# One tuned two-layer encoder kernel: the openings' PSUM bank pairs, the norm's scaled copy, the split of the late row tile and the first down group are changed

## Chip, cores and metric

The kernel runs on one core of a Trainium2 chip. The metric is the device time of one execution in microseconds (us), as the median of several runs. The engines are named as the profile names them: PE (TensorE, matmul), DVE (VectorE), ACT (ScalarE), POOL (GpSimd) and SP (SyncE, which here only issues DMAs).

## What is computed

512 frames and 16 meta tokens (528 tokens of 1024 channels, fp32) pass two layers; each layer is a half-weighted SwiGLU FFN, a mixer and a second FFN. Cut to what matters here:

```python
def swiglu(x, w_gate, w_up, w_down):
    return (jax.nn.silu(x @ w_gate) * (x @ w_up)) @ w_down
...
    for l in range(DEPTH):
        h = h + 0.5 * swiglu(rmsnorm(h, ffn1_norm[l]), ffn1_w_gate[l], ffn1_w_up[l], ffn1_w_down[l])
        h = h + hybrid_mixer(rmsnorm(h, mix_norm[l]), w_in[l], ...)
        h = h + 0.5 * swiglu(rmsnorm(h, ffn2_norm[l]), ffn2_w_gate[l], ffn2_w_up[l], ffn2_w_down[l])
    h = rmsnorm(h, final_norm)
    return h[:, N_META:]
```

The mixer projects to q, k, v, two convolution halves a and b, and two gates; it runs a stick-breaking attention and a causal depthwise convolution and merges both. D_FF is 2816, so an FFN has 22 row tiles of 128 hidden channels.

## The kernel before

**Precision.** Activations lie transposed, 128 channels by 528 tokens a tile. Every fp32 operand is split into a high part (a cast to fp32r, by ScalarE, line 80) and a low part (the difference, by VectorE, line 81); a product is three matmuls: high by high, high by low, low by high. Weights arrive by DMA as `wr` (256 to 512 KB each) and are split into `wh` and `wl`, four buffers each, in `prep_unit` (lines 254 to 289). `unit` (291) hands out the split weights in the order in which TensorE uses them and splits `LOOK` = 3 units ahead. For most units of the mixer the low part is made in another way (lines 265 to 268): ScalarE writes the cast, then a negated copy of the raw weight's part, and a DMA on POOL's queue adds to it; only q's first weight tile takes the plain split.

**Order.** A scheduler orders each engine's instructions ahead of time by priorities; `priority(-URGENT)` moves something forward, and a manual dependency without a semaphore only fixes an order on one engine. `follow` (249) uses such a dependency to keep a weight split behind the last instruction that TensorE waits for, kept in `ahead`. Within openings and first down groups TensorE's order is written by hand.

**Openings.** Products of pairs of row tiles use seven products in place of eight (a 2 by 2 block scheme over token halves and channel halves; w11, s1, s2, w21, s3, w22, s4). The first two pairs of an FFN, and a and b in the mixer, are interleaved in `pair` (lines 438 to 540): five openings in all, two in mixers and three in FFNs (the first FFN has a head of its own, `first_head`). PSUM has eight banks, used as four pairs under the tags ps (two), pb and pe. An opening begins with o11 for both row-tile pairs (`As`), while the norm's sum of squares is still being finished; it copies the first result into pb (`begin`), and lets TensorE form the norm's column sums (`between`, `rms_rstd`, 558). `rsqrt` (549) then makes the reciprocal root: Ln and Exp on ScalarE give a first value, and one Newton step on VectorE uses a scaled copy of the sums (line 553). After that come o21, s1, s2, o21, w22, s3, s1, s2, s4, s3, w22, s4. `evict` (677), or `take` in the mixer (956), empties a PSUM pair: gate by rstd, silu or sigmoid, up by gate.

**Down products.** After the first 4, 10, 16 and 22 row tiles an FFN runs `down` (799): eight output tiles in the order 0, 4, 1, 5, 2, 6, 3, 7, each a sum over the group's row tiles. Only the last group's result goes straight to h; the others are scaled by rstd on VectorE (816) and added by POOL (818). A row tile whose product came out last waits in `late`; its split (`parts`, 642) is done at the start of `down`. So that TensorE has something to do meanwhile, the first two or, after an opening, three output tiles are begun together and take the late row tiles last (lines 821 to 835).

Of the kernel before, what the change touches and what calls it, by code (L numbers as in the profile page):

```python
# [61 lines left out]
def kernel(ctx, tc, hT, par, const, wg1, wu1, wd1, win, wao, wco, wout, wg2, wu2, wd2, out):  # L62
# [108 lines left out]
                units += [((f"d{fi}", l, gi, j), wd[l, j, :, m0:m1], m1 - m0) for j in ORDER]  # L171
    LOOK = 3
    RAW = 3
    state = {"prep": 0, "use": 0, "fetch": 0, "out": 0, "sums": 0, "look": LOOK}
    ready, raws, counted = {}, {}, set()
    quads = {"pool": None, "of": None}

# [76 lines left out]
    def prep_unit():  # L254
        n = state["prep"]
        key, src, nk = units[n]
        state["prep"] += 1
        fetch()
        hi = wpool.tile([P, 8, P], F32R, tag="wh", bufs=4, name="wh")
        lo = wpool.tile([P, 8, P], F32R, tag="wl", bufs=4, name="wl")  # L260
        ready[key] = (hi, lo)
        if nk not in QUAD:
            raw, nk0, nk = raws[key], nk, 8 if nk in OPEN else nk
            if key[0] in MIXER and key[0] + str(key[2]) != "q0" or nk0 == "o21" and units[n - 1][2] == "o11":
                act.copy(hi[:, :nk], raw[:, :nk])  # L265
                act.activation(lo[:, :nk], raw[:, :nk], AF.Copy, scale=-1.0)
                for a, b, src in pieces(n):
                    pool.dma_start(lo[:, a:b], src.bitcast(F32R), accum_op=ALU.add)
            else:
                split(raw[:, :nk], hi[:, :nk], lo[:, :nk])  # L270
            drop(key)
        else:
            at = key[1:]
            if at in opened:
                fetch_sums(WHEN.get((nk, units[n - 1][2]), 0))
            elif nk == "w11":
                fetch_sums(2)
            if nk == "s2" or nk == "s4" and at not in opened:
                x, y = raws[("s1", *at)], raws[("w22" if nk == "s2" else "w21", *at)]
                i = dve.tensor_tensor(out=x, in0=x, in1=y, op=ALU.add)  # L280
                if at in opened:
                    follow(i, "dve")
            pair_ = split(raws[("s1" if nk in ("s2", "s4") else nk, *at)], hi, lo)
            if at in opened:
                for i, engine in zip(pair_, ("act", "dve")):
                    follow(i, engine)
            for d in DONE[nk]:
                drop((d, *at))
        fetch()
# [148 lines left out]
    def pair(ptile, sp, st, mode, of, ats, between, take, done):  # L438
# [42 lines left out]
        def out(n, c, i, t):  # L481
            with priority(-URGENT):
                ahead["act"], ahead["dve"] = take(n, c, i, t)

        Bs = [ptile("pb")]
        As = [ptile() for _ in range(2)]
        ahead.clear()
        state["look"] = 1
        ws = [unit("o11", *of, at) for at in ats]
# [2 lines left out]
            products(As[n], ws[n], x(0, 0), True, ks)  # L492
        begin(Bs[0], v(As[0]))
        copy = ahead["act"]
        between(ptile("pe"), copy)

        Bs.append(kept(As[1], False))
        G, q, E, c22 = {}, {}, {}, {}
# [5 lines left out]
        def step(name, n):  # L504
            if (name, n) in (("w22", 0), ("s4", 0)):
                add_w21(int(name == "s4"))
            w = unit(name, *of, ats[n])
            if name == "o21":
                products(As[n], w, x(0, 1))
                (out if n else take)(n, As[n], 0, 0)  # L510
                if n:
                    keep, Bs[n], G[n] = Bs[n], ptile(), ptile()
                    begin(Bs[n], keep)
            elif name == "s1":
                if not n:
                    G[n] = ptile("pe")
                products(G[n], w, sx(0), True)
                q[n] = kept(G[n])
            elif name == "s2":
                products(Bs[n], w, sx(1))  # L520
                E[n] = ptile("pe")
                opposite(E[n], Bs[n], q[n])
            elif name == "s3":
                products(Bs[n], w, sx(2))
                c22[n] = sp.tile([P, 2, TH], F32, tag="c22", bufs=2, name="c22")
                opposite(c22[n], Bs[n], q[n])
                out(n, c22[n], 1, 1)
            elif name == "w22":
                products(E[n], w, sx(3))
                out(n, E[n], 1, 0)  # L530
            else:
                done(n, 1)
                products(Bs[n], w, x(1, 1))
                out(n, Bs[n], 0, 1)
                done(n, 0)
# [22 lines left out]
    def rms_rstd(tp, st, ps, mode, dst=None):  # L558

        if dst is None:  # L560
            dst = npool.tile([P, T], F32, tag="rstd", bufs=1, name="rstd")
        src = st["sum"]
        hi, lo = (tp.tile([P, T], F32R, tag="nt", bufs=3, name="nt") for _ in range(2))
        ahead["act"], ahead["dve"] = split(tri(src, mode), tri(hi, mode), tri(lo, mode))
        for pi, part in enumerate((hi, lo)):
            for b, s, w in ranges(mode):
                pe.matmul(ps[:, b, :w], onesm, part[:, s:s + w], start=(pi == 0), stop=(pi == 1))
        x, y = (tp.tile([P, T], F32, tag="nt", bufs=3, name="nt") for _ in range(2))
        rsqrt(sv(dst, mode), sv(x, mode), sv(y, mode), pv(ps, mode), -D, 1e-6, 0)
        return dst  # L570


# [52 lines left out]
    def ffn(l, fi, st, mode, after):  # L625
# [3 lines left out]
        with tc.tile_pool(name=f"ffn{l}{fi}", bufs=1, reuse_waits="tile") as fp, \  # L629
# [12 lines left out]
            def parts(u, m):  # L642
                if m >= GROUPS[-1][0]:
                    pool.tensor_tensor(out=tri(u, mode), in0=tri(u, mode), in1=tri(norm["r"], mode), op=ALU.mult)
                ah = fp.tile([P, T], F32R, tag="ah", bufs=6, name="ah")
                al = fp.tile([P, T], F32R, tag="al", bufs=6, name="al")
                split(tri(u, mode), tri(ah, mode), tri(al, mode))
                a_parts[m] = (ah, al)

            def plain(tag, key, m, between=None):  # L650

# [61 lines left out]
            def first_head():  # L713

                ws = [tuple(wpool.tile([P, 8, P], F32R, tag=n, bufs=4, name=n) for n in ("wh", "wl")) for _ in begin]
                pss = [ptile(t) for t in ("ps", "ps", "pb")]
                for name in ("s1", "s3"):
                    fetch(quads["pool"].tile([P, 8, P], F32, tag=name, bufs=2, name=name))
                for a, b in BEGIN:
                    for k in range(a, b):  # L720
                        prepare(fp, k, 0, st, alloc="later")
                    for raw, (hi, lo) in zip(begin, ws):
                        split(raw[:, a:b], hi[:, a:b], lo[:, a:b])
                    for k in range(a, b):
                        squares(fp, k, st, mode)
                    if b == KD:
                        fetch()
                        fetch_sums(2)
                        nc.sync.dma_start(prm[:, N_NORM:], par[:, N_NORM:])
                        norm["r"] = npool.tile([P, T], F32, tag="rstd", bufs=1, name="rstd")  # L730
                        rstd_from(fp, st["sum"], ptile("pe"), D, 1e-6, 0, mode, norm["r"])
                    for k in range(a, b):
                        xh, xl = st["u"][k]
                        for ps, (hi, lo) in zip(pss, ws):
                            for pi, (wt, xt) in enumerate(((hi, xh), (hi, xl), (lo, xh))):
                                for e, s in enumerate(toks):
                                    pe.matmul(ps[:, e, :TH], wt[:, k, :], xt[:, s], start=(k == 0 and pi == 0),
                                              stop=(k == KD - 1 and pi == 2))
# [60 lines left out]
            def down(gi, opened=False, tp=None):  # L799
                with priority(-opened * URGENT):  # L800
                    while late:
                        parts(*late.pop())
                m0, m1 = GROUPS[gi]
                last = gi == len(GROUPS) - 1
                xs = [a_parts[m] for m in range(m0, m1)]
                nk = m1 - m0
                tags = ("ps", "ps", "pb", "pe")

                def update(j, pd):
                    if last:  # L810
# [8 lines left out]


                ws, pds = [], []
                if opened:
                    tags = ("ps", "pb", "pe", "ps")
                n0 = 3 if opened else 2
                for n in range(n0):
                    state["look"] = LOOK - n * opened
                    ws.append(unit(f"d{fi}", l, gi, ORDER[n]))
                    pds.append(ptile(tags[n]))
                state["look"] = LOOK
                with tc.manual_schedule(engines={mybir.EngineType.PE}) if opened else nullcontext():  # L830
                    for ks in (range(nk - 2), (nk - 1,), (nk - 2,)):
                        for j in range(n0):
                            gemm(pds[j], ws[j], 0, nk, xs, mode, ks, nk - 2)
                for n in range(n0):
                    update(ORDER[n], pds[n])
                for n, j in list(enumerate(ORDER))[n0:]:
                    if last and after is finish_prepare and n == KD - 2:
                        finish(tp, ptile, [unit(f"d{fi}", l, gi, j) for j in ORDER[n:]], nk, xs)
                        break
                    pd = ptile(tags[n % 4])  # L840
                    gemm(pd, unit(f"d{fi}", l, gi, j), 0, nk, xs, mode)
                    update(j, pd)

# [519 lines left out]
```

## Time and profile before

| | |
|---|---|
| runs, median | 2143.83 us (2143.65 to 2146.93, 3 runs) |
| the profiled execution | 2141.3 us |
| its span, first to last instruction | 2139.5 us |
| granted TensorE clock | 0.999 |
| matmuls | 16058 |
| DMA moved | 334.34 MB, mean 156 GB/s |

The profile is one execution. Its rows give start, length, engine, line of the kernel, operation and `out<-in` by the program's names (buffer numbers left out), the partitions by elements, and in brackets how long the engine had been idle and what ended that. A row with x2 is two instructions merged. Matmul ends are modelled, and matmuls overlap: a matmul of 264 columns has a length of 0.28 us but the next one may start after 0.12. In the mixer's openings the tags ps, pb and pe appear as bs, bb and be.

### The profile page before, as it was taken

The numbers are of one execution on the slowest core, as the hardware profiler recorded it, in microseconds if no ns is written. First come the engines' busy times: TensorE is split into PE (matmuls) and PEld (weight loads), VectorE is DVE, ScalarE is ACT, GpSimd is POOL, SyncE is SP. The second block draws the span as 40 slices with busy tenths as digits, with TensorE's granted clock in tenths as the row PEclk, the third lists the DMA queues.
The fourth block names the chain that finished last, engine by engine and source line by source line (L and its number), as shares of the span: only waits on it lengthen the run. The fifth ranks groups of instructions, "written<-read, shape, count | busy, mean of one in ns | idle before, by whom it ended". The sixth has DMA issues, their size and how long they took to land.

```text
span 2139.5 us, 39983 instructions
## 1 busy us (share of the span) xinstructions
PE 2118.2 (99%) x16058; PEld 2031.1 (95%) x16058; DVE 1600.1 (75%) x2233; ACT 1170.8 (55%) x1660; POOL 514.1 (24%) x477
## 2 busy tenths in 40 slices
PE   9999999999999999999999999999999999999998
PEld 9999999999999999999999999999888889899897
DVE  6867688788876777677797676887788768767685
ACT  6434356677776645343564343566778776444354
POOL 1322321311111141323123223213212112322220
PEclk9999999999999999999999999999999999999999
DMA  7465538665568867464386655385656788665542
GB/s 227 137 165 142 145 104 227 165 134 125 131 172 182 206 169 180 125 164 119 99 210 167 165 144 143 104 223 157 150 121 140 182 186 208 179 178 143 144 110 78
DMA packets 152121, 334.34 MB, mean 156 GB/s; under 512 B 16896, under 2 KB 21120, under 8 KB 151936
## 3 DMA queue, kind: packets, MB, share of 16 engines
q1 hardware_dynamic: 110928, 235.27, 33.9%
q0 software_dynamic: 40320, 95.96, 26.2%
q8 instruction: 126, 2.06, 0.4%
q10 hardware_dynamic: 688, 0.55, 0.1%
q14 instruction: 59, 0.48, 0.1%
HBM read 325.30 MB, written 6.42 MB: 155 GB/s over the span
## 4 chain that ended last, share of the span: by engine, by line
PE 88%; DVE 5%; DMA 4%; ACT 1%; issue 1%; POOL 0%; SPq 0%; DVEq 0%; ACTq 0%; POOLq 0%
PE ps L761 15%; PE pb L761 14%; PE ps L906 13%; PE ps L308 11%; PE ps L892 10%; PE pb L308 6%; PE pe L308 5%; PE pe L761 5%; DMA wl<-win 1%; DVE wl L81 1%; PE ps L459 1%; PE z L1091 1%; PE po L1135 1%; PE z L1114 1%; PE bb L459 1%
## 5 line engine op out<-in xcount | busy, mean ns | idle before, releaser
L80 ACT CAST wh<-wr 128x1024 fp32r<-128x1024 f32 (+4 forms) x296 | 263.8, 898 | 344.8 <-PE ps L308 91.8
L81 DVE TENSOR_TENSOR wl<-wr,wh 128x1024 fp32r<-128x1024 f32 (+4 forms) x296 | 331.5, 1124 | 64.8 <-ACT wh L80 62.3
L80 ACT CAST wh<-s 128x1024 fp32r<-128x1024 f32 x171 | 179.3, 1048 | 261.4 <-DVE s L280 87.4
L81 DVE TENSOR_TENSOR wl<-s,wh 128x1024 fp32r<-128x1024 f32 x171 | 233.0, 1363 | 49.1 <-ACT wh L80 48.0
L818 POOL TENSOR_TENSOR h<-h,dt 128x528 f32<-128x528 f32 (+1 forms) x96 | 176.9, 1850 | 257.2 <-DVE dt L816 256.5
L906 PE MATMUL ps<-uh,wh 128*128 128x264 f32 (+1 forms) x664 | 207.5, 312 | 0.0
L906 PE MATMUL ps<-uh,wl 128*128 128x264 f32 (+1 forms) x664 | 203.7, 307 | 0.7 <-DMA wl<-win 0.7
L906 PE MATMUL ps<-ul,wh 128*128 128x264 f32 (+1 forms) x664 | 203.7, 307 | 0.0
L210 POOL DMA_DIRECT2D s<-wg x81 | 72.0, 889 | 524.9 <-DMA s<-wg 312.8
L935 DVE SCALAR_TENSOR_TENSOR y<-uc,prm,y 128x528 f32<-128x528 f32 (+1 forms) x240 | 184.4, 806 | 0.5
L761 PE MATMUL ps<-ul,wh 128*128 128x264 f32 (+1 forms) x576 | 163.7, 284 | 0.0
L761 PE MATMUL pb<-sl,wh 128*128 128x264 f32 (+1 forms) x576 | 163.3, 283 | 0.0
L761 PE MATMUL ps<-uh,wl 128*128 128x264 f32 (+1 forms) x576 | 163.2, 283 | 0.0
L761 PE MATMUL pb<-sh,wl 128*128 128x264 f32 (+1 forms) x576 | 163.2, 283 | 0.0
L761 PE MATMUL pb<-sh,wh 128*128 128x264 f32 (+1 forms) x576 | 162.9, 283 | 0.0
L761 PE MATMUL ps<-uh,wh 128*128 128x264 f32 (+1 forms) x576 | 162.6, 282 | 0.0
L308 PE MATMUL ps<-ah,wh 128*128 128x264 f32 (+1 forms) x616 | 142.2, 301 | 1.5 <-ACT ah L80 1.5
L308 PE MATMUL ps<-al,wh 128*128 128x264 f32 (+1 forms) x616 | 142.2, 300 | 1.0 <-DVE al L81 0.9
L308 PE MATMUL ps<-ah,wl 128*128 128x264 f32 (+1 forms) x616 | 141.8, 300 | 0.0
L265 ACT CAST wh<-wr 128x1024 fp32r<-128x1024 f32 x91 | 95.4, 1049 | 84.3 <-PE ps L906 36.3
L906 PEld LDWEIGHTS ps<-uh,wl 128*128 128x128 f32 x664 | 125.0, 188 | 7.0 <-DMA wl<-win 1.1
L906 PEld LDWEIGHTS ps<-uh,wh 128*128 128x128 f32 x664 | 124.9, 188 | 5.4
(404 smaller groups left out, 6836.8 us busy)
## 6 DMA issues: line engine op xcount, KB each, us to landing
wr<-wd SPq DMA_DIRECT2D x96, 384.0 KB, 3.6
wr<-wg SPq DMA_DIRECT2D x129, 256.0 KB, 3.1
wr<-wu SPq DMA_DIRECT2D x129, 256.0 KB, 3.6
wr<-win SPq DMA_DIRECT2D x56, 512.0 KB, 3.9
wl<-win POOLq DMA_DIRECT2D x54, 512.0 KB, 7.9
s<-wg SPq DMA_DIRECT2D x87, 256.0 KB, 5.1
s<-wu SPq DMA_DIRECT2D x87, 256.0 KB, 5.5
s<-wg POOLq DMA_DIRECT2D x81, 256.0 KB, 5.1
```

What stands on the lines that cost most here:

```text
L80: i = act.copy(hi, x)
L81: return i, dve.tensor_tensor(out=lo, in0=x, in1=f(hi), op=ALU.subtract)
L210: queue.dma_start(raw[:, a:b], src, **kw)
L265: act.copy(hi[:, :nk], raw[:, :nk])
L308: pe.matmul(ps[:, c, :n], wt[:, k0 + k, :], xt[:, s:s + n], start=(k == 0 and pi == 0), stop=(k == end and pi == 2))
L459: pe.matmul(ps[:, e, :TH], wt[:, 4 * e + kk, :], xt, start=start and kk == 0 and pi == 0, stop=kk == KH - 1 and pi == 2, skip_group_check= ...
L761: pe.matmul(ps[:, e, :TH], wt[:, 4 * e + kk, :], xt, start=start and kk == 0 and pi == 0, stop=kk == 3 and pi == 2, skip_group_check=True)
L818: pool.tensor_tensor(out=tri(h[j], mode), in0=tri(h[j], mode), in1=tri(t, mode), op=ALU.add)
L892: pe.matmul(ps, wt[:, k0 + k, :], xt[:, s], start=(n == 0 and pi == 0), stop=(n == nk - 1 and pi == 2))
L906: pe.matmul(ps, wt[:, k, :], xt[:, s], start=(n == 0 and pi == 0), stop=(n == KD - 1 and pi == 2))
L935: t = dve.scalar_tensor_tensor(out=y, in0=uc[i][:, c0 + k:k + T], scalar=col(w0 + k), in1=y, op0=ALU.mult, op1=ALU.add)
L1091: pe.matmul(z[:, hh, :n], kk[r, ks], qq[r, q0:q0 + n], start=(pi == 0), stop=False, skip_group_check=True)
```

## The change

- **Bank pairs.** In `pair` the first opening tile moves from ps to pe, the norm's sums from pe to ps, s1's and s2's result tiles from pe to ps, and the copied tile of the second row-tile pair from ps to pe. `down` uses the pairs in the order ps, ps, pb, pe, also after an opening; the last group uses ps, ps, pe, pb. `first_head` names pb and pe before ps.
- **Norm.** `rms_rstd` no longer calls `rsqrt`: the scaled copy of the sums is made by ScalarE, from PSUM, between Ln and Exp, with the factor 0.5; the constants of the Newton step are arranged to fit. Other users of `rsqrt` are as before.
- **Late row tile.** `parts` returns the two instructions of its split; `down` keeps them in `ahead`, and weight units that are split while the first tiles of an opened down group are requested follow behind them.
- **First down group.** It begins three output tiles together in every FFN, the first FFN too; there the row tiles come in the order 0, 1, then 2, then 3.
- **k's first weight tile** takes the plain split. **s3's eviction** in an opening is no longer urgent and no longer what later splits follow.

```diff
@@ prep_unit
-            if key[0] in MIXER and key[0] + str(key[2]) != "q0" or nk0 == "o21" and units[n - 1][2] == "o11":
+            if key[0] in MIXER and key[0] + str(key[2]) not in ("q0", "k0") or nk0 == "o21" and units[n - 1][2] == "o11":
...
-                split(raw[:, :nk], hi[:, :nk], lo[:, :nk])
+                pair_ = split(raw[:, :nk], hi[:, :nk], lo[:, :nk])
+                if state["behind"]:
+                    for i, engine in zip(pair_, ("act", "dve")):
+                        follow(i, engine)
@@ pair
-        As = [ptile() for _ in range(2)]
+        As = [ptile(), ptile("pe")][::-1]
...
-        between(ptile("pe"), copy)
+        between(ptile(), copy)
...
-                    keep, Bs[n], G[n] = Bs[n], ptile(), ptile()
+                    keep, Bs[n], G[n] = Bs[n], ptile("pe"), ptile()
...
-                    G[n] = ptile("pe")
+                    G[n] = ptile()
...
-                E[n] = ptile("pe")
+                E[n] = ptile()
...
-                out(n, c22[n], 1, 1)
+                take(n, c22[n], 1, 1)
@@ rms_rstd
-        rsqrt(sv(dst, mode), sv(x, mode), sv(y, mode), pv(ps, mode), -D, 1e-6, 0)
+        r, x, y, ps = sv(dst, mode), sv(x, mode), sv(y, mode), pv(ps, mode)
+        fn(r, ps, AF.Ln, bias=bias[:, 0:1], scale=-1.0 / D)
+        act.activation(x, ps, AF.Copy, scale=0.5 / D)
+        fn(r, r, AF.Exp, bias=B_ZERO, scale=-0.5)
+        dve.tensor_tensor(out=y, in0=r, in1=r, op=ALU.mult)
+        dve.scalar_tensor_tensor(out=y, in0=x, scalar=-0.5e-6, in1=y, op0=ALU.add, op1=ALU.mult)
+        dve.scalar_tensor_tensor(out=r, in0=y, scalar=1.5, in1=r, op0=ALU.add, op1=ALU.mult)
@@ parts
-                split(tri(u, mode), tri(ah, mode), tri(al, mode))
                 a_parts[m] = (ah, al)
+                return split(tri(u, mode), tri(ah, mode), tri(al, mode))
@@ first_head
-                pss = [ptile(t) for t in ("ps", "ps", "pb")]
+                pb, pe_ = ptile("pb"), ptile("pe")
+                pss = [ptile(), ptile(), pb]
@@ down
-                        parts(*late.pop())
+                        ahead["act"], ahead["dve"] = parts(*late.pop())
+                state["behind"] = opened
...
-                tags = ("ps", "ps", "pb", "pe")
+                tags = ("ps", "ps", "pe", "pb") if last else ("ps", "ps", "pb", "pe")
...
-                if opened:
-                    tags = ("ps", "pb", "pe", "ps")
-                n0 = 3 if opened else 2
+                n0 = 2 if gi else 3
                 for n in range(n0):
-                    state["look"] = LOOK - n * opened
+                    state["look"] = LOOK - n * (gi == 0)
...
-                state["look"] = LOOK
+                state.update(look=LOOK, behind=False)
+                order = (range(nk - 2), (nk - 2,), (nk - 1,)) if first and gi == 0 else (range(nk - 2), (nk - 1,), (nk - 2,))
...
-                    for ks in (range(nk - 2), (nk - 1,), (nk - 2,)):
+                    for ks in order:
                         for j in range(n0):
-                            gemm(pds[j], ws[j], 0, nk, xs, mode, ks, nk - 2)
+                            gemm(pds[j], ws[j], 0, nk, xs, mode, ks, order[-1][0])
```

More of the change, by code (lines that the diff above doesn't have):

```diff
@@ L173 @@
     RAW = 3
-    state = {"prep": 0, "use": 0, "fetch": 0, "out": 0, "sums": 0, "look": LOOK}
+    state = {"prep": 0, "use": 0, "fetch": 0, "out": 0, "sums": 0, "look": LOOK, "behind": False}
     ready, raws, counted = {}, {}, set()
@@ L730, in first_head @@
                         norm["r"] = npool.tile([P, T], F32, tag="rstd", bufs=1, name="rstd")
-                        rstd_from(fp, st["sum"], ptile("pe"), D, 1e-6, 0, mode, norm["r"])
+                        rstd_from(fp, st["sum"], pe_, D, 1e-6, 0, mode, norm["r"])
                     for k in range(a, b):
@@ L839, in down @@
                         break
-                    pd = ptile(tags[n % 4])
+                    pd = ptile(tags[n % len(tags)])
                     gemm(pd, unit(f"d{fi}", l, gi, j), 0, nk, xs, mode)
```

## The prediction

> **What bounds the kernel now.** I read the busy line of the page first, then the table of waits of TensorE (engine and line, what it waited for, total us, times, longest), then the timelines round each wait.
>
> ```profile
> PE 2118.2 (99%) x16058; PEld 2031.1 (95%) x16058; DVE 1600.1 (75%) x2233; ACT 1170.8 (55%) x1660; POOL 514.1 (24%) x477
> ```
>
> ```profile
> PE ps L737 <- ACT wh L80: 4.7, 1, 4.7
> PE ps L761 <- DVE dt L816: 1.6, 2, 0.8
> PE ps L308 <- ACT ah L80: 1.5, 3, 0.9
> PE ps L308 <- DVE al L81: 0.9, 3, 0.4
> PE bs L459 <- DVE wl L81: 0.9, 1, 0.9
> PE ps L906 <- DMA wl<-win: 0.7, 2, 0.4
> PE bs L459 <- ACT bb L472: 0.5, 2, 0.3
> PE ps L459 <- DVE h L1292: 0.5, 1, 0.5
> PE be L459 <- DVE nt L553: 0.4, 1, 0.4
> PE pe L459 <- DVE nt L553: 0.4, 1, 0.4
> ```
>
> TensorE works 99% of the span and the change adds and removes no matmul, so nothing can be won but its idle time: 2139.5 − 2118.2 = 21.3 us, of which these ten rows of the table name 12.1 and the first, 4.7, is the start of the kernel. The change aims at the rows of L816, ah, al, wl L81, L906, L1292 and the two of L553: 1.6 + 1.5 + 0.9 + 0.9 + 0.7 + 0.5 + 0.4 + 0.4 = 6.9 us in 2 + 3 + 3 + 1 + 2 + 1 + 1 + 1 = 14 waits.
>
> A wait costs more than its idle time, because the matmuls overlap. TensorE's timeline (start, length) round the wait of the first k:
>
> ```profile
> 416.97 0.29 PE L906 MATMUL ps<-uh,wh 128*128 128x264 f32 x1
> 417.09 0.28 PE L906 MATMUL ps<-ul,wh 128*128 128x264 f32 x1
> 417.72 0.39 PE L906 MATMUL ps<-uh,wl 128*128 128x264 f32 x1 [0.34 <-DMA wl<-win]
> 417.95 0.28 PE L906 MATMUL ps<-uh,wh 128*128 128x264 f32 x1
> ```
>
> Running, matmuls start 0.12 us apart. Here one starts 0.63 after the last and the next 0.23 after it: (0.63 − 0.12) + (0.23 − 0.12) = 0.62 lost for 0.34 idle. So each wait is priced at its idle time + **0.28**; the 14 waits are worth 6.9 + 14 × 0.28 = 10.8 us. That is the most that the aimed-at waits can give.
>
> **The change, part by part.**
>
> *Bank pairs (2.9).* In the first down group of an opened FFN, tile 7 now lies in pe and not in ps. VectorE and TensorE at the first pair of row tiles after it, second FFN:
>
> ```profile
> 1150.62 0.70 DVE L816 SCALAR_TENSOR_TENSOR dt<-ps,rstd 128x528 f32<-128x528 f32 x1
> 1151.47 0.36 PE L761 MATMUL ps<-sh,wh 128*128 128x264 f32 x1 [0.78 <-DVE dt L816]
> ```
>
> The pair's second ps tile waits until the last down tile is evicted at 1151.3. With tile 7 in pe, that ps pair holds tile 5, done two tiles (6 us) earlier; pe is wanted only after two more products. Both L816 waits go: 1.6 + 2 × 0.28 = 2.1. The opening's first tile moves from ps to pe. After the mixer of layer 0 the ps pair still waits for h L1292, while pe lies on the banks of the LayerNorm sums, long free; the second opening tile, now in ps, starts 18 matmuls (2.2 us) later, after that eviction. 0.5 + 0.28 = 0.8. Before other openings nothing is paid: the last down group swaps pb and pe, so that pe is done one tile (4.4 us) before the opening starts, and pb is written only by a copy some 6 us into it. Cover gone, each would cost one eviction, 0.70.
>
> *The norm's copy (1.0).* ScalarE round the norm of the mixer in layer 0, and the reader on VectorE:
>
> ```profile
> 375.36 0.59 ACT L465 COPY q<-bs 128x528 f32<-128x528 f32 x1
> 375.85 0.70 ACT L104 ACTIVATE rstd<-be,bias 128x528 f32<-128x528 f32 x1
> 376.44 0.63 ACT L80 CAST sh<-g 128x528 fp32r<-128x528 f32 x1
> 376.96 0.74 ACT L104 ACTIVATE rstd<-rstd,bias 128x528 f32<-128x528 f32 x1
> 377.91 1.05 ACT L80 CAST wh<-wr 128x1024 fp32r<-128x1024 f32 x1 [0.20 <-DVE wr L280]
> 378.98 1.28 ACT L100 ACT_TABLE_LOAD   x1
> ```
>
> ```profile
> 377.79 0.70 DVE L553 TENSOR_SCALAR nt<-be 128x528 f32<-128x528 f32 x1
> ```
>
> The tile of s1 takes the pair that the norm's sums held, before and after the change (now ps, whose other half the second opening tile holds). It is free when the last reader is done: L553, at 378.5, after a wait of 0.4, so that TensorE was ready at 378.1. The new readers are Ln (done 376.55) and a ScalarE copy, for which I take the 0.59 of L465, the same shape out of the same kind of pair (ends: 0.5, and 0.74 of the longest activation here). Done by 377.2 (376.55 + 0.59), or 377.7 behind the cast. Both L553 waits go: 0.8 + 2 × 0.28 = 1.4. Exp and all behind it on ScalarE comes 0.6 later, VectorE is 0.70 lighter, so rstd is no later. What is late next: s2 starts 0.7 earlier and its low weights are then some 0.1 to 0.3 short in this mixer; with a restart I deduct 0.4. Net 1.0.
>
> A row against a rule: L465 took 0.59, L553 0.70, both 128x528 out of a pair. The Trainium skill ("ScalarE: Activation LUTs", section "Rules for kernel authors") gives multiplications to VectorE, up to about 3 times faster there in bf16; this trace, in fp32 from PSUM, has it the other way.
>
> *The late row tile (2.7).* ScalarE, VectorE and TensorE at the first down group of the last FFN:
>
> ```profile
> 1829.24 0.62 ACT L80 CAST wh<-wr 128x512 fp32r<-128x512 f32 x1 [4.08 <-DMA wr<-wd]
> 1829.76 0.41 ACT L104 ACTIVATE g<-g 128x256 f32<-128x256 f32 x1
> 1830.95 0.62 ACT L80 CAST ah<-up 128x512 fp32r<-128x512 f32 x1 [0.77 <-DVE up L682]
> ```
>
> ```profile
> 1825.81 0.42 DVE L680 TENSOR_TENSOR g<-ps,rstd 128x256 f32<-128x256 f32 x1
> ```
>
> ```profile
> 1831.62 0.50 PE L308 MATMUL ps<-ah,wh 128*128 128x512 f32 x1 [0.94 <-ACT ah L80]
> ```
>
> ScalarE stood 4.08 us at the head cast of the fourth down tile, whose DMA was late; the gate of the late row tile was ready at 1826.2 and waited behind it. That cast is the one split which the change ties behind the late tile: the look-ahead has split the first three already. Freed of it, what is left of the chain is 0.41 (gate), a product as long as L680's 0.42, ah's 0.62 and al's 0.7: 2.2 us, from 1826.2 to 1828.4; were it twice as long it would end by 1830.6, before TensorE asks for ah at 1830.7 (1831.62 − 0.94). The tied cast waits for its DMA anyway (to 1829.2), and its low part is done about 1.3 later, at 1830.6 (0.62 + 0.7); the fourth tile starts 18 half-width matmuls (2.2 us) after TensorE asks for ah, at 1832.9. The same picture stands in the second FFN. Of the 2.4 us in the ah and al rows 0.76 are the first FFN's (next part); the other 1.64, in four waits, go: 1.64 + 4 × 0.28 = 2.7. The wait that is added, fourth split behind al, holds up only later weight casts on ScalarE, which wait for a free buffer until TensorE has used tile one.
>
> *First down group with three tiles (1.3).* In the very first FFN:
>
> ```profile
> 57.61 0.51 PE L308 MATMUL ps<-ah,wh 128*128 128x264 f32 x2 [0.31 <-ACT ah L80]
> 58.57 0.51 PE L308 MATMUL ps<-al,wh 128*128 128x264 f32 x2 [0.45 <-DVE al L81]
> ```
>
> ```profile
> 53.24 0.69 DVE L81 TENSOR_TENSOR wl<-wr,wh 128x512 fp32r<-128x512 f32 x1
> ...
> 57.81 0.70 DVE L81 TENSOR_TENSOR al<-up,ah 128x528 fp32r<-128x528 f32 x1
> ```
>
> TensorE asks for row tile 3, finished last, at 57.3, two tiles of 12 matmuls (2.9 us) after the group's start at 54.4. Now three tiles take row tiles 0 and 1 and then 2: 3 × 1.46 + 3 × 0.73 = 6.6 us, so 61.0, against al at 58.5. Gain 0.31 + 0.45 + 2 × 0.28 = 1.3. The third tile's weights, split by 53.9, are there.
>
> *k's first weights (1.3).* Instead of cast, negated copy and an adding DMA, now cast and VectorE subtraction.
>
> ```profile
> 408.61 9.06 DMA wl<-win
> ```
>
> ```profile
> 406.94 1.22 DVE L81 TENSOR_TENSOR wl<-wr,wh 128x1024 fp32r<-128x1024 f32 x1
> ```
>
> The DMA took 9.06 us and TensorE waited for it; a subtraction is 1.22 (that of q's weights), put where VectorE then waits over 2 us for TensorE. Ready near 409.5, wanted at 417. Two layers: 0.7 + 2 × 0.28 = 1.3. ScalarE and the POOL queue lose a copy and a DMA, which only helps v's.
>
> *s3's eviction no longer urgent (0.9).* In the mixer of layer 1:
>
> ```profile
> 1463.97 0.82 DVE L963 TENSOR_TENSOR tmp<-c,rstd 128x264 f32<-128x264 f32 x1
> 1464.71 1.37 DVE L964 TENSOR_TENSOR uc<-c,rstd 128x264 f32<-128x264 f32 x1
> 1466.00 1.21 DVE L81 TENSOR_TENSOR wl<-s,wh 128x1024 fp32r<-128x1024 f32 x1
> ```
>
> The split may now pass L963 and L964: done 2 us earlier, and 0.9 + 0.28 = 1.2 goes. The next split waits for a sum that comes by DMA; I deduct 0.3. If the order stays, the term is nothing.
>
> **Sum.** 2.9 + 1.0 + 2.7 + 1.3 + 1.3 + 0.9 = 10.1; call it 10.0. The profiled execution took 2141.3 (span 2139.5, 1.8 around it), so 2131.3; the runs' median, 2143.83, stands 2.5 above it, so **2133.8** for the median.
>
> **Rivals.**
>
> *DMA becomes the bound.* The window of the second layer's first FFN opening, with its first down group (length, busy us of PE, PEld, DVE, ACT, POOL, then clock, DMA share, GB/s):
>
> ```profile
> 1075.00:1133.00 58.00, 57.44 (x469) 56.81 (x468) 47.63 (x77) 34.43 (x54) 15.69 (x19) 1.00 0.91 223
> ```
>
> At 0.91 there is little room. For: the fourth down tile was late already. Against: 9% of 58 us is 5, and no opening shrinks by more than 3. If all that the FFN openings and their down groups win (2.9 + 0.7 + 2.7 = 6.3) is lost to later landings, 3.7 is left: 2140.1. If half, 6.9: 2136.9.
>
> *Slower: the copy stands too late on ScalarE.* If the scheduler puts it behind Exp, the next 1.05 us cast and the 1.28 us table load, it ends near 380.9 (after the load's end at 380.3) instead of 377.7, and TensorE, whose order is fixed by hand, ready at 378.1, stands at s1 for 2.8 + 0.28 = 3.1 in all five openings: 15.4, against 10.1 − 1.0 = 9.1 won: 2143.8 + 6.3 = 2150.1. It decides from the point where the copy ends after 378.1. Against: it reads what Ln reads and stands ahead of Exp in the program.
>
> *The tie misses.* If the cast that blocks is not the one tied, 2.7 stays: gain 7.3, 2136.5.
>
> *The copy itself is slow.* If it took over 1.55 us (378.1 − 376.55), twice the longest activation here, the wait of s1 would stay: the 1.0 goes, 2134.8. L465's 0.59 speaks against it. The Trainium skill's rule above is on its side.
>
> **How the numbers follow.** Forecast (7 to 12.5 won, 2131.3 to 2136.8; the low end leaves out the terms of the norm's copy, of s3 and 1.2 for splits that come late; the high end adds the undeducted 0.7 and the waits of bb, 0.5 + 0.56) 0.61, with the slow copy 0.02 and the missed tie 0.04 at its edge; half lost to DMA 0.14; all of it lost, or new waits of the same size, 0.10; slower 0.06; still faster than the forecast's range 0.03. A measurement here can tell about 0.2%, 4.3 us, from no change: faster 0.61 + 0.02 + 0.04 + 0.14 + 0.03 = 0.84, same 0.10, slower 0.06. For 8 in 10 the range takes in the forecast, the tie and half the DMA case, and part of the last: 2130.5 to 2140.0.
>
> **What would show it.** Right: the rows of L816, L553, L1292 and wl<-win at L906 leave the table of waits, ah and al all but leave it, TensorE's idle time falls to 21.3 − 6.9 = 14.4 us, the fourth down tile's cast stands behind ah on ScalarE. Wrong: new rows of DMA or ACT releasers at L459 or L308 with idle sums of several us, or a DMA share at 1.0 in the openings.

## The result and the profile after

| | before | after |
|---|---|---|
| median of five runs, us | 2143.83 (2141.22 to 2146.93) | 2135.67 (2134.28 to 2139.23) |
| after over before | 1 | 0.9967 [0.9956, 0.9978] |
| profiled execution, us (span) | 2141.3 (2139.5) | 2139.23 (2137.5) |

The ratio says 7.1 us faster, with an interval from 4.7 to 9.4. The profiled execution of after is the slowest of its five; a second profile of the same kernel, below, ran in 2134.38. After's busy line, and its table of TensorE's waits (engine, line, what it waited for, total us, times, longest):

```profile
PE 2116.6 (99%) x16058; PEld 2031.3 (95%) x16058; DVE 1595.7 (75%) x2230; ACT 1170.3 (55%) x1663; POOL 513.2 (24%) x475
```

```profile
PE ps L747 <- ACT wh L80: 4.9, 1, 4.9
PE pe L462 <- DVE wl L81: 2.3, 3, 0.8
PE pe L462 <- DVE ps L481: 1.3, 3, 0.5
PE pe L462 <- ACT wh L80: 1.3, 2, 0.8
PE be L462 <- DVE bs L481: 1.2, 1, 1.2
PE bs L462 <- DVE wl L81: 0.6, 2, 0.3
PE be L462 <- ACT bb L475: 0.5, 2, 0.3
```

(L747 here is L737 of before, L462 is L459, L481 is L478.) All but one of the rows that the change aimed at have left: the down tiles' eviction, ah and al, the h of the LayerNorm, the DMA of k's weights, the norm's nt. The one left is the mixers' wl (bs), 0.9 in one wait before and 0.6 in two now. There are five rows at L462, the openings' products, with 2.3 + 1.3 + 1.3 + 1.2 + 0.6 = 6.7 us in 11 waits: low and high weights (wl, wh) and two evictions. None was in before but one wl wait of 0.9. So TensorE's idle time was 2137.5 − 2116.6 = 20.9, where 14.4 was forecast; in the faster second profile it was 16.5.

**Where the new waits come from.** In the opening of layer 0's second FFN the products of w22 for the second pair stood twice, for its cast (wh) and its low part (wl). Timeline of after, VectorE's sum that these weights are made from, and TensorE:

```profile
748.84 1.23 DVE L283 TENSOR_TENSOR s<-s,wr 128x1024 f32<-128x1024 f32 x1 [1.78 <-DMA wr<-wu]
...
751.28 0.40 PE L462 MATMUL pe<-sh,wh 128*128 128x264 f32 x1 [0.51 <-ACT wh L80]
...
752.53 0.39 PE L462 MATMUL pe<-sh,wl 128*128 128x264 f32 x1 [0.75 <-DVE wl L81]
```

The sum waited for a load, wr<-wu. In before the same sum started without a wait at 747.60:

```profile
747.60 1.22 DVE L280 TENSOR_TENSOR s<-s,wr 128x1024 f32<-128x1024 f32 x1
```

The load is issued by SP, which goes through its list in order. SP's timeline, before and then after:

```profile
739.75 0.33 SPq L210 DMA_DIRECT2D wr<-wg  x1
740.12 0.68 SPq L210 DMA_DIRECT2D wr<-wu  x1
741.23 0.34 SPq L210 DMA_DIRECT2D s<-wg  x1
741.61 0.50 SPq L210 DMA_DIRECT2D s<-wu  x1
```

```profile
737.52 0.33 SPq L210 DMA_DIRECT2D s<-wg  x1
737.89 0.45 SPq L210 DMA_DIRECT2D s<-wu  x1
739.00 0.33 SPq L210 DMA_DIRECT2D wr<-wg  x1
739.37 0.55 SPq L210 DMA_DIRECT2D wr<-wu  x1
```

The two loads have changed places. Before, wr<-wu landed 6.7 us after its issue; after, 9.4 us, with the half megabyte of s issued 1.5 us ahead of it (739.00 − 737.52). The order alone does not make it that late: in the second profile of the same kernel (run 1 below), with the same order, it landed after 6.7 us, and TensorE did not wait in this opening. What sets the order is when the buffers come free on VectorE, whose timelines (before, then after) show the split that frees wr and the addition that frees s:

```profile
738.50 1.22 DVE L81 TENSOR_TENSOR wl<-wr,wh 128x1024 fp32r<-128x1024 f32 x1
...
739.98 1.22 DVE L502 TENSOR_TENSOR wr<-wr,s 128x1024 f32<-128x1024 f32 x1
```

```profile
736.28 1.22 DVE L505 TENSOR_TENSOR wr<-wr,s 128x1024 f32<-128x1024 f32 x1
...
737.76 1.21 DVE L81 TENSOR_TENSOR wl<-wr,wh 128x1024 fp32r<-128x1024 f32 x1
```

Split, then addition before; addition, then split after. The split ends at 739.72 in before and wr is issued at 739.75; the addition ends at 737.50 in after and s is issued at 737.52.

### The profile page after: what moved, and what is told of

Same layout as the page of the kernel before. It is cut to its first block, busy times and chain, and to the rows that moved or that the text cites. A ratio compares the mean times of both kernels' runs of the same rounds, so it can differ in the third digit from the quotient of the medians.

```text
span 2137.5 us, 39987 instructions
## 1 busy us (share of the span) xinstructions
PE 2116.6 (99%) x16058; PEld 2031.3 (95%) x16058; DVE 1595.7 (75%) x2230; ACT 1170.3 (55%) x1663; POOL 513.2 (24%) x475
## 4 chain that ended last, share of the span: by engine, by line
PE 91%; DVE 4%; DMA 3%; ACT 1%; issue 1%; SPq 0%; DVEq 0%; POOL 0%; ACTq 0%; POOLq 0%
PE pb L771 15%; PE ps L771 15%; PE ps L916 13%; PE ps L311 12%; PE ps L902 10%; PE pe L311 6%; PE pb L311 5%; PE pe L771 5%; DMA wr<-wu 1%; PE z L1101 1%; DMA s<-wg 1%; PE po L1145 1%; DVE wl L81 1%; PE z L1124 1%; PE pe L462 1%; PE be L462 1%
```

## The experiments

Two theories of the new waits. **Order:** the scheduler, with the norm's copy gone from VectorE, puts the first addition of w21 (L505) ahead of the second o21's low split; SP then issues s ahead of wr in the openings, and w22's weights are late. **Bandwidth** (the prediction's rival): TensorE merely comes earlier to loads that take what they take. Each run is timed in rounds with the kernel before on the same chip; before's median there was 2142.7, 2142.26, 2142.79 and 2142.44 in the four groups (runs 1 to 4, 5 to 8, 9 to 11, 12).

**1. The changed kernel once more.**

> The changed kernel once more, so that the others have it on the same chip. Order theory (the norm's copy on ScalarE lets VectorE add w21 earlier, which turns round two loads on SP's queue; the openings' new waits come from that) and bandwidth theory (the new waits come from TensorE arriving earlier at DMAs that move 90% of what they can) both expect about 0.9967 of the kernel before, 2133 to 2139 us, and again waits of some 6 us in all at L462, behind wl, wh and the second row-tile pair's copy L481.

Measured: 2134.57 (2134.08 to 2137.39), 0.9967 [0.9955, 0.998]. Its profile has the evictions at L481 for 0.8 in two waits and a wl wait of 0.8, where after's had 1.3 and 2.3; both theories had some 6 us of waits again, so the new waits come and go with the run. With after's five runs the kernel has ten, median 2135.28, from 2134.08 to 2139.23; that is the base below.

**2. The changed kernel without the norm's copy on ScalarE.**

```diff
-        fn(r, ps, AF.Ln, bias=bias[:, 0:1], scale=-1.0 / D)
-        act.activation(x, ps, AF.Copy, scale=0.5 / D)
...
+        rsqrt(sv(dst, mode), sv(x, mode), sv(y, mode), pv(ps, mode), -D, 1e-6, 0)
```

> The changed kernel with the norm's scaled copy back on VectorE (rsqrt). Order theory: the loads of SP stand as before, the waits at L462 behind wl, wh and L481 in the second half of the openings (5.3 us idle in 11 waits in the profile of after) go, the two waits of 0.4 behind L556's reader at s1 come back: net 4 to 7 us faster than after, 2127 to 2132 us. Bandwidth theory: TensorE is within 1 us as early, the new waits stay, and with s1's waits the kernel is about 1 us slower than after, 2136 to 2140 us.

Measured: 2133.51 (2132.05 to 2133.95), 0.9957 [0.9945, 0.997]. The nt waits are back (0.8 and 0.3) and the wl and wh waits have gone; of the evictions at L481 one wait of 0.6 is left. (The expectation's 5.3 us for the new waits is 6.7 by the table above.) All five runs lie below all ten of the changed kernel: the norm's copy costs 1.8 there, or 1.1 beside run 1 alone, though the waits that it was to remove are removed. The direction is that of the order theory; its size, 4 to 7 us, is missed.

**3. The changed kernel with the addition tied behind the split.**

```diff
+                if nk0 == "o21":
+                    state["o21"] = pair_[1]
...
-            dve.tensor_tensor(out=x, in0=x, in1=y, op=ALU.add)
+            i = dve.tensor_tensor(out=x, in0=x, in1=y, op=ALU.add)
+            if not n:
+                tc.add_manual_dep(i.ins, state["o21"].ins.name, NOSYNC, reason="behind o21's split")
```

> The changed kernel, norm's copy on ScalarE, but the first addition of w21 tied on VectorE behind the low part of the second o21's weights, so that in the FFN openings SP sends w22's load ahead of the sum's load as before. Order theory: the FFN openings lose their new waits (0.5 + 0.75 + 0.47 us idle in the first of them), and nothing comes back at s1: 4 to 7 us faster than after, 2127 to 2132 us; in the mixers, where the order is only half restored, part stays. Bandwidth theory: no change from after beyond 1 us.

Measured: 2133.04 (2132.38 to 2133.99), 0.9956 [0.9942, 0.9969]; again all five below all ten. SP's queue has wr (738.56) ahead of s (740.04) again, and the waits of the FFN openings are gone; four waits for evictions stay, all in the mixers' openings:

```profile
PE be L464 <- DVE bs L483: 1.2, 2, 0.7
PE bs L464 <- DVE bs L483: 0.7, 2, 0.3
```

The same bytes are moved, so bandwidth alone can't have made the waits. The gain is 2.2 (1.5 beside run 1 alone), and the order theory's 4 to 7 is missed here too.

TensorE's 16058 matmuls come in the same order in runs 1 and 3, so the two profiles can be lined up matmul by matmul. Of SP's 765 DMAs 20 differ in place, four in each of the five openings. Run 1 falls 2.0 and 0.8 us behind run 3 in layer 1's two FFN openings, 0.1 in layer 0's, where it did not wait, and 0.5 in the first FFN, where the two do not differ. It gains 0.8 and 1.4 in the mixers, where run 3 has its four waits, and ends 1.3 behind (2132.6 for 2131.3).

**4. The kernel before with the norm's copy alone** (the lines that run 2's diff takes out, put into before).

> The kernel before with the norm's copy on ScalarE and nothing else. Order theory: s1's waits (0.8 us idle in two, 1.4 with restarts) go, but the new waits at L459 behind wl, wh and the second pair's copy appear though TensorE arrives almost as late as before: 2 to 6 us slower than before. Bandwidth theory: 1 to 1.5 us faster than before, no new waits. The prediction's step: 1.0 faster.

Measured: 2145.16 (2139.88 to 2148.26, 11 runs), 1.0013 [1.0004, 1.0022]: 2.5 above the kernel before. Its profile is that of its fastest run. The nt rows are gone. Of these three rows the first two are new; the third was 0.9 in one wait in before:

```profile
PE pb L459 <- DVE wl L81: 1.0, 2, 0.6
PE ps L459 <- DVE wl L81: 0.9, 2, 0.5
...
PE bs L459 <- DVE wl L81: 0.6, 2, 0.3
```

VectorE and SP there, in the opening of layer 0's second FFN:

```profile
737.11 1.22 DVE L502 TENSOR_TENSOR wr<-wr,s 128x1024 f32<-128x1024 f32 x1
...
738.58 1.22 DVE L81 TENSOR_TENSOR wl<-wr,wh 128x1024 fp32r<-128x1024 f32 x1
```

```profile
738.35 0.33 SPq L210 DMA_DIRECT2D s<-wg  x1
...
739.83 0.46 SPq L210 DMA_DIRECT2D wr<-wg  x1
```

SP's order differs from before's in 20 places, four in each of the five openings. The first two rows' waits stand in layer 1's two FFN openings; in the opening shown, wr<-wu landed 6.3 us after its issue and TensorE did not wait. The one edit brings the swap and new waits with it, without any other part of the change having moved TensorE ahead.

**5. The changed kernel with the bank pairs as before.**

```diff
-        As = [ptile(), ptile("pe")][::-1]
+        As = [ptile() for _ in range(2)]
...
-                tags = ("ps", "ps", "pe", "pb") if last else ("ps", "ps", "pb", "pe")
+                tags = ("ps", "pb", "pe", "ps") if opened else ("ps", "ps", "pb", "pe")
```

> The changed kernel with the bank pairs of the openings and of the down groups as before (the first down group's three-tile tags too). The prediction's term for the pairs is 2.9 (L816 dt 2.1, h of the LayerNorm 0.8). If that term is right, both waits for dt come back with 0.8 us idle each and the wait for h with 0.5, and the median lies 2.9 above the changed kernel's 2134.6 to 2135.7: near 2138. If TensorE's earlier arrival only moves the waits to the weights (the DMA-bound rival), the idle time of the weight rows falls by about as much as dt's row rises and the time stays within 0.7 of the changed kernel's.

Measured: 2138.04 (2136.5 to 2141.93, 11 runs), 0.9984 [0.9975, 0.9993]: 2.8 above the changed kernel. The rows that the pairs were to remove are back, as long as in before:

```profile
PE ps L770 <- DVE dt L826: 1.5, 2, 0.8
...
PE ps L462 <- DVE h L1301: 0.5, 1, 0.5
```

**6. The kernel before with the late row tile's tie and the three tiles alone.**

```diff
-                        parts(*late.pop())
+                        ahead["act"], ahead["dve"] = parts(*late.pop())
+                state["behind"] = opened
...
-                n0 = 3 if opened else 2
+                n0 = 2 if gi else 3
```

> The kernel before with two parts of the change alone: the split of the fourth down tile tied behind the late row tile, and three output tiles in the first down group. The prediction's terms are 2.7 + 1.3 = 4.0, so the median should be 4.0 below the kernel before: near 2138.7 with the shared runs at 2142.7; the ah and al rows of TensorE's waits (2.4 us in 6 waits in before) all but go, the dt, nt and win rows stay, and no new weight wait stands in the openings, since the order of the weight queue there is that of before (order theory). If the queue of transfers is the limit, new waits for wl or wh of some 1 to 3 us show here as well and the gain is 2 or less.

Measured: 2137.4 (2135.61 to 2138.73, 11 runs), 0.9974 [0.9965, 0.9983]: 4.9 below. No ah or al row is left, and no new weight row; dt stands as in before, and nt with three waits for two:

```profile
PE ps L764 <- DVE dt L820: 1.5, 2, 0.8
PE be L462 <- DVE nt L556: 0.9, 2, 0.4
```

**7. The changed kernel with k's first weights the old way.**

```diff
-            if key[0] in MIXER and key[0] + str(key[2]) not in ("q0", "k0") or nk0 == "o21" and units[n - 1][2] == "o11":
+            if key[0] in MIXER and key[0] + str(key[2]) not in ("q0",) or nk0 == "o21" and units[n - 1][2] == "o11":
```

> The changed kernel with the first weights of k split as before (cast, negated copy, adding DMA). The prediction's term is 1.3: the two waits at L906 for the DMA of wl come back with 0.3 to 0.4 us idle each, and the median rises by 1.3 to about 2136. If VectorE's extra subtraction of 1.22 us per layer displaces other work that TensorE waits for, the rise is under 0.5.

Measured: 2135.16 (2132.13 to 2137.83), 0.9968 [0.9955, 0.998]: not to be told from the changed kernel, though with such a range a term of 1.3 is not ruled out by the times. The waits for this DMA do not come back though the DMA does, so the term's mechanism is missed; the expectation's other reading had the size (under 0.5), for another reason. GpSimd's queue issued it before the product uc, not behind it as in before:

```profile
407.78 0.87 POOL L268 DMA_DIRECT2D wl<-win  x1 [3.36 <-ACT wl L266]
408.59 0.75 POOL L977 TENSOR_TENSOR uc<-uc,tmp 128x264 f32<-128x264 f32 x1
```

In before it was issued at 408.61 (its row is in the prediction), right after such a product, and was 0.34 late. Here it goes 0.8 us earlier while TensorE began q's products 0.4 earlier (410.72 for 411.12), so that 0.4 is gained, enough for it to be there. Which other part of the change moved the issue is not shown.

**8. Run 3's kernel with s3's eviction urgent again.**

```diff
-                take(n, c22[n], 1, 1)
+                out(n, c22[n], 1, 1)
```

> The changed kernel with the first addition of w21 on VectorE put behind the low-part split of the second o21 (as in the run that gave 2133.04), and the eviction of s3 urgent again as before. If the term of s3 is right (0.9), the time is 0.9 above that run's, near 2133.9, with a wait for wl at the second halves of the mixers' openings. If the not-urgent eviction only changes which work stands late on VectorE, the wait for wl takes the place of the waits for bs of the eviction (0.7 to 1.2 us idle in that run) and the time is within 0.4 of 2133.0.

Measured: 2134.07 (2132.44 to 2135.48), 0.9961 [0.9949, 0.9974]: 1.0 above run 3, as the term of 0.9 has it, though the two ranges overlap. Its profile, of its slowest run, has the eviction in the mixers at 1.8 + 0.6 and wl waits of 0.5 and 0.3.

**9. Run 4's kernel with run 3's tie.**

> The kernel before with the norm's scaled copy by ScalarE alone (that was 2145.16 beside 2142.7), and the first addition of w21 put behind the second o21's low-part split on VectorE. With that the queue of weight loads goes in the order of before again in all five openings. If the lost order is the whole cost of the copy (order theory), the wl waits in the openings' second halves go, the nt waits stay away, and the copy gives the gain that the prediction gave it: about 1.0 below the kernel before, 3.5 below 2145. If the cost is in the copy itself (ScalarE 0.59 longer ahead of its casts, Exp later), the time stays near 2144 to 2146 and the wl waits stay.

Measured: 2144.3 (2139.55 to 2147.02, 12 runs), 1.0001 [0.9992, 1.001]. A miss for the number: the order theory had about 2141.8. The wl waits fell from 2.5 to these, but others grew:

```profile
PE ps L308 <- ACT ah L80: 2.6, 2, 1.8
...
PE ps L912 <- DMA wl<-win: 1.2, 2, 0.6
PE bs L459 <- DVE wl L81: 0.9, 2, 0.5
...
PE pb L459 <- DVE wl L81: 0.5, 1, 0.5
```

By the ratios the tie gave back most of the 0.13% that run 4 lost, by the medians a third (0.9 of 2.5). The edit does less than the expectation says: SP's order is that of before again in the three FFN openings, while in each mixer one pair of loads stays swapped. The ah and win waits, which before has too (1.5 and 0.7), vary from run to run; in this kernel nothing removes them. The longest, 1.8 for ah, stands in the first FFN, ahead of every opening: lined up with before, this profile is 3.9 us behind after 800 matmuls and 3.6 at the end. That accounts for the one profile, not for the median; what is left of the copy's loss here is not settled.

**10. Run 3's kernel with two splits of each mixer's opening tied behind the eviction that the next products wait for.**

```diff
...
-                opposite(E[n], Bs[n], q[n])
+                opposite(E[n], Bs[n], q[n]); of[0] == 2 and (i := state.get((("w22", "s3")[n], *of, ats[n]))) and tc.add_manual_dep(i[1].ins, ahead["dve"].ins.name, NOSYNC, reason="behind E")
```

> The changed kernel with the addition behind the split (2133.04 in its run), and in the mixers' openings the low-part splits of w22 of the first pair and of s3 of the second put behind the eviction that the next products wait for. In that run four waits were left there, 0.33, 0.55, 0.32 and 0.69 us idle, with restarts 3.0 us. If they go and nothing takes their place: near 2130. If the split that now comes after the eviction is late instead, a wait for wl of up to 0.9 us (its 1.22 less the 0.3 of lead that is left) stands in the place of each, and the time is 2133 or more.

Measured: 2131.86 (2131.49 to 2136.88), 0.9954 [0.9941, 0.9967], the lowest median of all, 1.2 below run 3. The range takes in run 3's whole range, so by the times alone the gain is not shown, and the 2130 of the expectation is not reached. VectorE in the mixer of layer 1, in run 3 and here:

```profile
1465.31 1.22 DVE L81 TENSOR_TENSOR wl<-s,wh 128x1024 fp32r<-128x1024 f32 x1 [1.15 <-ACT wh L80]
1466.45 0.91 DVE L483 SCALAR_TENSOR_TENSOR bs<-be,q 128x264 f32<-128x264 f32 x2
```

```profile
1463.29 0.90 DVE L481 SCALAR_TENSOR_TENSOR bs<-be,q 128x264 f32<-128x264 f32 x2
1465.19 1.22 DVE L81 TENSOR_TENSOR wl<-s,wh 128x1024 fp32r<-128x1024 f32 x1 [0.99 <-ACT wh L80]
```

In run 3 VectorE idled 1.15 us for the split's cast while the eviction stood behind it; here the eviction fills that time. The four waits go (1.9 us idle), and two for wl of 0.3 each take the place of some: TensorE's idle time is 2129.7 − 2114.8 = 14.9. The edit also changed the place of one pair of SP's loads in each mixer.

**11. The kernel before with k's first weights alone** (run 7's diff, the other way, in before).

> The kernel before with k's first weights alone in the new way (cast and subtraction). The prediction's term is 1.3: both waits at L906 for the DMA of wl go (0.34 and 0.38 us idle) and the median lies 1.3 below the kernel before. If those waits are only there when the opening ahead ends early, as the changed kernel with the old way showed none of them, the rows of before's fresh runs decide: the gain is then under 0.5.

Measured: 2140.58 (2138.32 to 2142.31, 11 runs), 0.9988 [0.9979, 0.9996]: 2.2 below (0.9 to 4.5 by the ratio), and no DMA row at L906.

**12. Run 10's kernel with the copy on VectorE again** (run 2's diff). SP's list of 765 is the same in both.

> The kernel that gave 2131.86 (addition and mixers' splits tied) with the norm's scaled copy on VectorE again, as in the kernel before. The order of the weight queue is the same in both, so this is the copy without its side effect. The prediction priced it at 1.4 for two nt waits (0.4 us idle each) less 0.4. If that holds where the order is kept, the nt waits come back with some 0.4 us idle each, two to three of them, and the median is 1.0 to 1.4 above: near 2133. If the copy on ScalarE costs as much as it brings by its own length there, the time is within 0.5 of 2131.9 though the nt waits are back, or below it.

Measured: 2132.67 (2131.81 to 2133.71), 0.9953 [0.994, 0.9967]. The nt waits are back, in four places:

```profile
PE bs L462 <- DVE nt L556: 0.9, 2, 0.4
PE ps L462 <- DVE nt L556: 0.7, 2, 0.4
```

By the medians the copy brings 0.8 where the order is kept (2132.67 − 2131.86); the two ranges overlap and the ratios are alike, so it can be told neither from nothing nor from the 1.0 that was forecast.

**All fourteen profiles together.** Before, after and the twelve runs leave one profile each, with three openings of FFNs in each, 42 in all. SP issues wr and s in one order or the other, some 1.5 us or more apart; s is first in after and in runs 1, 4, 5 and 7, the ones with the copy on ScalarE and without a tie, and wr in all others. The landing of wr<-wu is counted from its issue, and a wait is one of TensorE in the 18 us after it:

| first on SP | openings | landing of wr<-wu, us: mean (range) | openings with a wait |
|---|---|---|---|
| wr | 27 | 7.22 (6.3 to 8.4) | 2 |
| s | 15 | 7.96 (6.3 to 9.4) | 13 |

The two openings without a wait where s is first had the two quickest landings there (6.3 and 6.7); the two with a wait where wr is first had landings among the slowest there (8.0 and 8.4). Of the kernels with the copy on ScalarE and the tie (runs 3, 8, 9 and 10) 2 of 12 openings have a wait, so it is the order and not the copy itself. The order decides in nearly every case, and the landing in the rest: by these figures the swap takes away the time that a slow landing needs.

## Why the prediction was right, and where it was wrong

The time came out 1.9 above the 2133.8, inside the range, and the gain was about 7 of the 10.0. It lies nearer to the rival with half the gain lost to DMA (2136.9) than to the forecast, so the time alone would not have told the two apart. (The high end of the forecast, 12.5, is mis-added: its own terms, 10.0 + 0.7 + 1.06, come to 11.8. Nothing here hangs on it.) By its own steps:

*Bank pairs (2.9).* Right: 2.8 when undone (3.6 by the ratios), with the very rows that were named.

*Late row tile (2.7) and three tiles (1.3).* Right: 4.9 for 4.0, which lies inside the interval of the ratio (3.6 to 7.5). ScalarE in the last FFN, after:

```profile
1825.48 0.42 ACT L104 ACTIVATE g<-g 128x256 f32<-128x256 f32 x1 [1.09 <-DVE g L689]
1826.39 0.62 ACT L80 CAST ah<-up 128x512 fp32r<-128x512 f32 x1 [0.49 <-DVE up L691]
1829.16 0.62 ACT L80 CAST wh<-wr 128x512 fp32r<-128x512 f32 x1 [2.15 <-DMA wr<-wd]
```

The gate goes at once, ah is done at 1827.0, and the cast that waits for its DMA stands behind it: the step as forecast. In before that cast held ah until 1831.6.

*k's first weights (1.3).* The waits went, but the term does not simply add. Alone it was worth 2.2, with 1.3 inside the interval; beside the other parts nothing that can be seen (2135.16 for 2135.28), and in that profile the old way's DMA is issued earlier and comes in time. The prediction took these waits as ones that only this part would end.

*s3 (0.9).* 1.0 beside run 3, not told from nothing by its range. In after the split does pass the two products as forecast (1462.31, with L973 at 1463.44), and the mixers' wl row fell from 0.9 to 0.6.

*The norm's copy (1.0).* **This is the step that failed**, and not at the copy. ScalarE round the norm of layer 0's mixer:

```profile
375.37 0.69 ACT L104 ACTIVATE rstd<-bs,bias 128x528 f32<-128x528 f32 x1
375.97 0.60 ACT L574 ACTIVATE nt<-bs 128x528 f32<-128x528 f32 x1
376.46 0.73 ACT L104 ACTIVATE rstd<-rstd,bias 128x528 f32<-128x528 f32 x1
```

It took 0.60 where 0.59 was taken from L465, stands right behind Ln, and the nt waits went: so the slow copy and the late copy, the slower rival among them, did not happen. What failed is "What is late next": the prediction looked at s2's weights, deducted 0.4, and left the order of everything else as it was. VectorE's list is made by a scheduler; with the copy gone from it an addition changed places with a split, the buffer that the addition frees changed the order of SP's loads, and w22's load was issued some 1.5 us behind another and landed 0.7 later on average. TensorE then waited in 13 of 15 FFN openings, where it did in 2 of 27 otherwise. The step cost 1.8 in the changed kernel (1.1 beside run 1 alone) and 2.5 alone (0.9 to 4.7 by the ratio), where 1.0 was to be won. By these runs the parts are 2.8 + 4.9 + 1.0 − 1.8 = 6.9 with nothing for k, beside 7.1 by the ratio; each of them is uncertain by a microsecond or more, so that the closeness is partly luck.

*DMA becomes the bound.* The half case (2136.9) lies 1.2 from the result, and the sign named for it, a new row of ACT at the openings' products, did appear, with 1.3 us and not several. The cause is mainly another: the window of before that the prediction quotes (0.91) reads the same in after,

```profile
1075.00:1133.00 58.00, 56.80 (x463) 56.20 (x462) 46.33 (x75) 33.99 (x53) 15.15 (x18) 1.00 0.91 223
```

and run 3 removed the FFN openings' waits with the same bytes in another order, run 4 made them without TensorE coming earlier. DMA still has a part in it, since the waits come and go with the landing times. That the order matters because DMA is 0.9 busy is argued, not shown: no run here moves fewer bytes.

The Trainium skill ("DMA: Bandwidth & Descriptors", section "Queues, rings and completion order") says that descriptors of one ring are taken in the ring's order, while completion is not in order by issuer. The traces fit it without showing the ring itself: wr landed 7.96 us after its issue where s went first and 7.22 where it did not, as means with overlapping ranges.

What stays open: why the tie gave only part of the loss back on before (run 9), and what made the scheduler move the addition. That the shorter path to rstd did it is argued, not shown.

## What to carry to other kernels

When an operation is moved between engines in a kernel whose order a scheduler makes, set the instruction lists of every engine and DMA queue of the two programs side by side, and price each pair that changed places, above all loads that one queue issues in turn in a stretch where DMA is 0.9 busy. A gain counted for a wait is good only while no other part of the change also ends that wait; price parts that touch one product together. When VectorE idles for a cast with an eviction right behind, try the eviction first: in run 10 it removed four waits, though the gain in time was not told from nothing.

## What the runs showed of the hardware that was not expected

The same program's waits at a late load differ from run to run: 6.7 us idle in 11 waits in one profile of the changed kernel (2139.23), 2.1 in five in another (2134.38). The two waits for the down tiles' eviction, dt, repeat: they came to 1.6 us in before and to 1.5 in the profiles of runs 4, 5 and 6. Not every wait for an eviction does: those at L481 in the openings came to 1.3 + 1.2 in one profile of the changed kernel and to 0.8 in the other. A price taken from one profile was firm for dt and not for those at L481 or at a late load.

A load's landing varies as much: the same 256 KB of wr<-wu, issued in the same order in the same kernel and opening, landed after 9.4 us in one profile and after 6.7 in another.
